# A mixer layer with three branches: splits of attention operands moved to GpSimd, earlier first loads, and new orders

## The chip, the cores and the metric

The kernel runs on one core of a Trainium2 chip. The metric is the device time of one execution in microseconds (us); lower is better. The profile of one execution gives the time of each instruction on each engine: TensorE (PE, with its weight loads as PEld), VectorE (DVE), ScalarE (ACT), GpSimd (POOL) and SyncE (SP), which issues nearly all DMAs here. PEclk, or granted clock, is the share of full speed that TensorE was given in a stretch.

## The reference

One layer with three parallel branches over 256 context tokens ("C") and 2048 latent tokens (a grid of 32 rows by 64 columns; four blocks of 512 tokens, L0 to L3).

```python
h = rmsnorm(x, g_pre) * (1.0 + scale) + shift          # scale, shift, gate = linear(silu(cond))
proj = h @ w_in                                        # 1024 -> 8208 columns
# A: gated DeltaNet, forward and backward, chunked, short conv on q, k, v; 4 heads of 128
# B: attention, 8 heads of 64: latents see an 8 x 16 neighbourhood plus all 256 context keys
#    in one softmax, with a bias table; context tokens see context tokens
# C: centred pooling with windows 2, 4, 8, 16, then a 128 x 128 product per group
y_na = o_na * silu(proj[..., OFF_NA_Z:OFF_PL_U])
merged = g_dn * (y_dn @ w_br_dn) + g_na * (y_na @ w_br_na) + g_pl * (y_pl @ w_br_pl)
out = x + gate * rmsnorm(merged @ w_out, g_post)
```

Outputs: both token sets, the context keys and values of branch B, and the final DeltaNet states of the context. Everything is in float32.

## The kernel before

A large product is made of three fp32r products: each operand is split into a high part (a cast to fp32r) and a low part (operand minus high part), and high-high, high-low and low-high are summed (`mm3`). So each operand needs a cast and a subtraction before TensorE can use it.

**Stages.** (1) Start: the modulation comes from `w_ada` in four parts of 2 MB (`ada_part`, q = 0 to 3, two tiles of 1 MB each, in a ring of three buffers), the inputs are normalised and transposed (`norm_x`, `turn`), and `make_h` writes the high and low part of h for C, L0 and L1. The first two weight units (`load_w`: 128 columns of `w_in`, two pieces of 256 KB, each with a cast and a subtraction on GpSimd) are loaded during q = 2 and q = 3. (2) `qkv` for C, L0, L1, then for L2, L3. (3) `rest`: the 40 other column units, first over C, L2, L3, then, after `reload_h` has fetched h of L0 and L1 again into the buffers of L2 and L3 (hL0 and hL1), over L0, L1. (4) `final`: the branch products, gates, output product and norm for L2, L3, L1, L0, C in turn; `final_y` loads and splits the branch outputs of a block (tiles yo, yh, yl).

**The side chain.** During `rest` the generator `branches` runs: gates of DeltaNet, preparation of 18 token tiles (`dn_prep`, `dn_invert`, `dn_merge`), the scan (`dn_scan`), then attention (`na_blocks`, `na_lane`, `na_pair`), then `final_y("L2")`, one after the other. Its matmuls are placed among the projections' by a hand-kept clock `self.t`: each matmul adds its modelled length, each piece of side work yields the model time at which it wants to go on, and `poll` emits it when that time has come. TensorE executes what results strictly in this order; the projections (tile mm, from hL0 and hL1) are the filler between side matmuls. The order of the other engines is made by a scheduler; loads issued through `dma_here` keep their order in SP's queue.

**The lines around the change.** `prep_load` starts the four loads of a tile and returns the model time at which the tile may be used:

```python
return Q, Qv, Es, self.t + 6
```

In attention, a group is one pair of heads with its keys (1536 latent and context columns, or 256 for C); it serves two blocks of queries (one for C), and a block is worked off in 4 jobs (2 for C) by three lanes. `na_pump` hands out loads whenever a buffer came free: queries of the next block, keys of the next group, values, bias tables, in that order, and again until nothing changes. Queries of a block are only asked for once the keys of its group have been. `split_part` loads up to 512 columns into a tile raw (two buffers) and splits them:

```python
self.nc.scalar.copy(hi, rv)
self.nc.gpsimd.tensor_tensor(lo, rv, hi.bitcast(F32), ALU.subtract)
self.use("s", n / 1000)
self.use("g", n / 400, self.t + 3)
```

`use` books modelled time on an engine; a block may start at the end of what is booked on GpSimd. At the end of a block its output oT is multiplied on GpSimd by the gate path z, for which raw is used once more, and stored.

Of the kernel before, what the change touches and what calls it, by code (L numbers as in the profile page):

```python
# [7 lines left out]
F32 = mybir.dt.float32  # L8
# [8 lines left out]
P = 128  # L17
# [30 lines left out]
class Net:  # L48
# [135 lines left out]
    def run(self):  # L184
        tc = self.tc
        with ExitStack() as st:
# [12 lines left out]
            with ExitStack() as s1:  # L199
                self.hp = pool(s1, "hp")  # L200
                self.wp = pool(s1, "wp", 3)
                with ExitStack() as s2:
                    self.ring("ax", s2, 6)
                    hcs = ExitStack()
                    self.dcs = ExitStack()
                    self.dc = phase(self.dcs, "dc", 1)
                    self.hc = phase(hcs, "hc", 1)
                    with ExitStack() as s3:
                        self.st = phase(s3, "st")
                        hA, hB = {}, {}  # L210
                        xp = phase(s3, "xp")
                        with ExitStack() as s4:
                            self.ap = phase(s4, "ada", 4)
                            self.xp, self.x_bufs = self.ap, 6
                            xc = self.norm_x(self.load_x("C", self.dma_here))
                            self.ada_start()
                            ws, tc_, t0, self.h0 = [], [], [], []
                            self.turn(xc, [xp.tile([P, D], F32, name="x", bufs=4) for _ in range(2)], tc_, range(KT))
                            hc = self.make_h("C", xc, hA, tc_)
                            for q in range(4):  # L220
                                self.ada_part(q)
                                if q == 0:
                                    x0 = self.norm_x(self.load_x("L0", self.dma_here))
                                    xt = [self.ap.tile([P, D], F32, name="xt") for _ in range(4)]
                                    h0 = self.make_h("L0", x0, hA, t0)
                                if q < 2:
                                    self.turn(x0, xt, t0, range(4 * q, 4 * q + 4))
                                else:
                                    ws.append(self.load_w(C_QKV + (q - 2) * P, self.dma_here))
                                for h in (hc, hc, h0, h0):  # L230
                                    next(h, None)
                            self.xp, self.x_bufs = xp, 4
                            x1 = self.load_x("L1", self.dma_here)
                            for h in (hc, h0):
                                next(h, None)
                            for k in range(KT):
                                self.dma_here(self.d_h["L0"][:, k, :], self.h0[k])
                            first = ws, [self.proj(w, hA["C"], CTX, self.ax1()) for w in ws]
                        self.lend(2)
                        self.more_consts()  # L240
                        self.qp = phase(s3, "qp")
                        self.norm_x(x1, tc.keep_in_program_order)
                        self.t += 6
                        self.add(self.make_h("L1", x1, hA), "h")
                        self.t -= 6
                        self.add(self.bias_tables())
                        self.qkv(hA, False, hB, first)
                        self.drain()
                        self.qkv(hB, True, None)
                        self.drain()  # L250
                    self.ax_es = s2.pop_all()
# [200 lines left out]
    def ada_part(self, q):  # L452

        nc = self.nc
        ps = self.mm_bank()
        for s in range(2):
            t = self.ap.tile([P, KT, 256], F32, name="w_ada", bufs=3)
            self.dma_here(t.rearrange("p k n -> p (k n)"), self.a["w_ada"][s, q])
            for k in range(KT):
                for c in range(2):  # L460
                    self.mm(ps[64 * s + 32 * c:64 * s + 32 * c + 32, :P], self.ada_sc[:, k, :], t[:, k, c * P:(c + 1) * P], k == 0, k == KT - 1)
        r = self.wp.tile([P, 4, P], F32, name="wraw", bufs=3)[:, 0]
        nc.scalar.copy(r, ps[:, :P])
        tp = self.ax1()[:, :P]
        self.tr(tp, r, self.ident)
# [334 lines left out]
    def prep_load(self, t):  # L800
# [8 lines left out]
        for d in (0, 1):  # L809
            E = dp.tile([P, 4, P], F32, name="E")  # L810
            self.dma(E, bass.AP(self.d_gr.tensor, self.d_gr.offset + (t * 8 + 4 * d) * P, [[0, P], [P, 4], [1, P]]))
            Es.append(E)
        return Q, Qv, Es, self.t + 6

    def dn_prep(self, t, ti, ub, Ms, ld):
        nc, dp = self.nc, self.dp
# [321 lines left out]
    def rest(self, h, blocks):  # L1138
# [4 lines left out]
        groups = [units[0:2]] + [[u] for u in units[2:-2]] + [units[-2:]]  # L1143
        for g in groups:
            ws = [self.load_w(u[0]) for u in g]
            for b in blocks:
                for w, (_, out, args) in zip(ws, g):
                    out(self.proj(w, h[b], BLK[b]), b, BLK[b], *args)

# [98 lines left out]
    def split_part(self, srcs, hi, lo, view=lambda x: x):  # L1248

        n = sum(s.shape[-1] for s in srcs)  # L1250
        raw = self.np.tile([P, 512], F32, name="raw", bufs=2)
        c = 0
        for s in srcs:
            self.dma(raw[:, c:c + s.shape[-1]], s)
            c += s.shape[-1]
        rv = view(raw[:, :n])
        self.nc.scalar.copy(hi, rv)
        self.nc.gpsimd.tensor_tensor(lo, rv, hi.bitcast(F32), ALU.subtract)
        self.use("s", n / 1000)
        self.use("g", n / 400, self.t + 3)  # L1260

    def na_blocks(self):

        self.blocks, self.groups = [], []
        for base, rbs in ((None, ("C",)), (0, (0, 1)), (12, (2, 3))):
            for hp in range(4):
                g = dict(base=base, hp=hp, left=len(rbs) * (2 if base is None else 4), ready=1e9)
                for rb in rbs:
# [9 lines left out]
    def na_pump(self):  # L1278

        while True:  # L1280
            n = self.group_n, self.block_n, self.v_n, self.tab_n
            g, b = self.group_n, self.block_n
            if b < len(self.blocks) and (b < 2 or self.blocks[b - 2]["scored"] == self.blocks[b - 2]["jobs"]):
                if self.blocks[b]["g"]["ready"] < 1e9:
                    self.na_queries(self.blocks[b])
                    self.block_n += 1
            if g < len(self.groups) and (g < 2 or self.groups[g - 2]["left"] == 0) and self.block_n >= (0, 1, 2, 3, 4, 6, 8, 10, 12, 14, 16, 18)[g] - 1:
                self.na_keys(self.groups[g])
                self.group_n += 1
            if self.v_n < len(self.v_queue):  # L1290
                old = self.v_queue[self.v_n - VBUFS] if self.v_n >= VBUFS else None
                if old is None or old[0]["read"][old[1]] == 2:
# [70 lines left out]
    def na_pair(self, lane, b, cb):  # L1363
# [101 lines left out]
        b["done"] += 1  # L1465
        if b["done"] == b["jobs"]:
            d = "C" if rb == "C" else f"L{rb}"
            while (1, hp, d) not in self.z_there:
                yield self.t + 1
            z = np_.tile([P, 512], F32, name="raw", bufs=2)[:, :BLK[d]]  # L1470
            self.dma(z, self.d_z[d][1, :, hp, :])
            nc.gpsimd.tensor_tensor(oT[:, :BLK[d]], oT[:, :BLK[d]], z, ALU.mult)
            self.dma(self.d_o[1, d][:, hp, :], oT[:, :BLK[d]])
        self.na_pump()

# [12 lines left out]
    def final_y(self, b, dma=None):  # L1488
# [3 lines left out]
        for bi in range(3):  # L1492
            yh = f.tile([P, 4, 512], F32R, name=f"yh{bi}", bufs=1)
            yl = f.tile([P, 4, 512], F32R, name=f"yl{bi}", bufs=1)
            for k in range(4):
# [5 lines left out]
                else:  # L1501
                    src = self.d_pl["L"][k, :, int(b[1]) * 512:(int(b[1]) + 1) * 512]
                dma(o[:, :n], src)
                if bi == 2:
                    z = f.tile([P, 512], F32, name="yz")
                    dma(z[:, :n], self.d_z[b][bi, :, k, :])
                    self.nc.gpsimd.tensor_tensor(o[:, :n], o[:, :n], z[:, :n], ALU.mult)
# [160 lines left out]
```

## Time and profile before

| | us |
|---|---|
| median of 3 runs | 2852.83 (2845.39 to 2856.17) |
| the profiled execution's own time | 2854.77 |
| its span | 2853.1 |
| TensorE busy in the span | 2764.9 (97%) |
| VectorE, ScalarE, GpSimd busy | 1477.3, 875.6, 1163.5 |

The span is what the trace covers; the execution's own time is 1.7 us longer. The mean granted clock is 0.987. TensorE's busy time is the union of its matmuls, whose ends are modelled. 64% of the span on the chain that ended last is TensorE at line 167 (all matmuls) on tiles mm, ax and sx; tile ax holds products of DeltaNet and some projections, sx those of attention, fo the output product.

### The profile page before, as it was taken

How to read it: one execution, taken by the hardware profiler on the slowest of the kernel's cores; microseconds unless marked ns; L12 is line 12 of the kernel's file. 1: busy time of each engine (PE TensorE's matmuls, PEld its weight loads, DVE VectorE, ACT ScalarE, POOL GpSimd, SP SyncE). 2: the span in 40 equal slices, each digit the busy share in tenths (PEclk: the TensorE clock that was granted, in tenths of full speed). 3: DMA queues.
4: the chain of work that ended last, by engine and by line, in shares of the span. 5: the costliest groups of instructions: out<-in, count | busy, mean ns of one | idle time of the engine just before them, and what ended most of it. 6: DMA issues, size and time to landing. Idle time of an engine off the chain costs nothing.

```text
span 2853.1 us, 49537 instructions
## 1 busy us (share of the span) xinstructions
PE 2764.9 (97%) x18254; PEld 2348.7 (82%) x18254; DVE 1477.3 (52%) x3128; ACT 875.6 (31%) x2145; POOL 1163.5 (41%) x1478
## 2 busy tenths in 40 slices
PE   6999999999999999999899999899999999999998
PEld 5888998888788888888788988688878877778887
DVE  6750055201488564655724665266666636446445
ACT  5221132112333232313223355344444422121112
POOL 4523233431334243323422056543333246656643
PEclk9999999999999999999999999999999999999999
DMA  7745423433555363645458986555555366556544
GB/s 285 212 137 174 144 98 96 119 96 112 184 166 158 122 214 108 202 126 161 142 184 302 313 281 215 177 156 151 168 148 159 108 207 233 184 174 217 175 156 135
DMA packets 354116, 492.26 MB, mean 173 GB/s; under 512 B 74921, under 2 KB 192721, under 8 KB 352849
## 3 DMA queue, kind: packets, MB, share of 16 engines
q1 hardware_dynamic: 353872, 489.09, 53.9%
q8 instruction: 144, 2.36, 0.3%
q14 instruction: 100, 0.81, 0.1%
HBM read 347.13 MB, written 155.60 MB: 176 GB/s over the span
## 4 chain that ended last, share of the span: by engine, by line
PE 73%; DMA 8%; DVE 8%; issue 3%; POOL 3%; ACT 2%; SPq 1%; POOLq 0%; ACTq 0%; DVEq 0%
PE mm L167 35%; PE ax L167 24%; PE sx L167 5%; PE fo L167 4%; PE sx L171 3%; PE ax L171 1%; DVE tm L917 1%; DVE Y L918 1%; DMA yo<-d_o0L 1%; DMA d_of<-o 1%; DMA yo<-d_o1L 1%; DMA raw<-d_nkL 1%; DVE mt L891 1%; DMA yz<-d_zL 1%; SPq L151 1%
## 5 line engine op out<-in xcount | busy, mean ns | idle before, releaser
L585 POOL CAST whi<-wraw 128x512 fp32r<-128x512 f32 x240 | 157.5, 657 | 625.2 <-PE ax L167 320.9
L167 PE MATMUL mm<-hL0h,whi 128*128 128x512 f32 x784 | 326.0, 416 | 2.9 <-ACT hL0h L181 2.9
L586 POOL TENSOR_TENSOR wlo<-wraw,whi 128x512 fp32r<-128x512 f32 x240 | 319.6, 1333 | 15.0
L167 PE MATMUL mm<-hL0l,whi 128*128 128x512 f32 x784 | 309.1, 394 | 1.6 <-POOL hL0l L182 1.6
L167 PE MATMUL mm<-hL0h,wlo 128*128 128x512 f32 x784 | 309.2, 394 | 0.0
L167 PE MATMUL mm<-hL1h,whi 128*128 128x512 f32 x472 | 197.7, 419 | 3.8 <-ACT zc L1155 3.8
L167 PE MATMUL ax<-hL1h,whi 128*128 128x512 f32 x488 | 195.4, 400 | 0.0
L167 PE MATMUL ax<-hL1l,whi 128*128 128x512 f32 x488 | 191.6, 393 | 1.8 <-DVE hL1l L548 1.1
L167 PE MATMUL ax<-hL1h,wlo 128*128 128x512 f32 x488 | 191.1, 392 | 0.0
L167 PE MATMUL mm<-yh,br_l 128*128 128x512 f32 (+1 forms) x480 | 179.2, 373 | 9.5 <-POOL br_l L1535 8.6
L167 PE MATMUL mm<-hL1h,wlo 128*128 128x512 f32 x472 | 186.0, 394 | 0.0
L167 PE MATMUL mm<-hL1l,whi 128*128 128x512 f32 x472 | 185.9, 394 | 0.0
L167 PE MATMUL mm<-yh,br_h 128*128 128x512 f32 (+1 forms) x480 | 178.0, 371 | 2.0 <-DVE gt L1542 1.0
L167 PEld LDWEIGHTS mm<-hL0h,whi 128*128 128x128 f32 x784 | 149.2, 190 | 35.4 <-issue 5.6
L167 PE MATMUL mm<-yl,br_h 128*128 128x512 f32 (+1 forms) x480 | 177.8, 370 | 0.0
L167 PEld LDWEIGHTS mm<-hL0h,wlo 128*128 128x128 f32 x784 | 148.6, 190 | 32.5
L167 PEld LDWEIGHTS mm<-hL0l,whi 128*128 128x128 f32 x784 | 149.4, 191 | 27.4 <-POOL hL0l L182 2.1
L1535 POOL TENSOR_TENSOR br_l<-br_r,br_h 128x512 fp32r<-128x512 f32 x104 | 149.6, 1450 | 0.7
L1408 DVE CUSTOM_DVE_ANT_0 pr<-sx,tab 128x736 f32<-128x736 f32 (+2 forms) x128 | 105.7, 863 | 81.7 <-PE sx L167 72.7
L1410 ACT ACTIVATE pr<-pr,mx 128x736 f32<-128x736 f32 (+2 forms) x128 | 109.5, 856 | 109.2 <-DVE mx L1408 109.0
L167 PE MATMUL fo<-woh,mh 128*128 128x512 f32 x288 | 113.9, 396 | 7.2 <-DVE fy L1581 7.2
L167 PEld LDWEIGHTS mm<-yh,br_l 128*128 128x128 f32 x480 | 91.8, 191 | 27.7 <-POOL br_l L1535 11.5
(383 smaller groups left out, 6787.4 us busy)
## 6 DMA issues: line engine op xcount, KB each, us to landing
wraw<-w_u SPq DMA_DIRECT2D x240, 256.0 KB
br_r<-w_br SPq DMA_DIRECT2D x120, 256.0 KB
d_gL<-th SPq DMA_DIRECT2D x96, 256.0 KB
gt<-d_gL SPq DMA_DIRECT2D x96, 256.0 KB
skv<-d_kv SPq DMA_DIRECT2D x36, 512.0 KB
d_zL<-zc SPq DMA_DIRECT2D x48, 256.0 KB
tab<-d_tab SPq DMA_DIRECT2D x48, 240.0 KB
V<-d_nvL SPq DMA_DIRECT2D x128, 80.0 KB
```

Of the source, the lines that this page charges most:

```text
L151: return self.nc.sync.dma_start(out, in_)
L167: self.nc.tensor.matmul(out, lhsT=l, rhs=r, start=start, stop=stop)
L171: self.nc.tensor.transpose(out, in_, ident)
L585: self.nc.gpsimd.tensor_copy(h, raw)
L586: self.nc.gpsimd.tensor_tensor(l, raw, h.bitcast(F32), ALU.subtract)
L891: v.transpose(mt[q, h], M[q, h, q])
L917: v.tensor_tensor(tv, U[:n, 0:i, i:i + 1].broadcast_to([n, i, w]), Y[:n, i:i + 1, i:32].broadcast_to([n, i, w]), ALU.mult)
L918: v.tensor_tensor(Y[:n, 0:i, i:32], Y[:n, 0:i, i:32], tv, ALU.subtract)
L1408: nc.vector.tensor_tensor_reduce(out=pr[:, :nk], in0=ps[:, :nk], in1=tab[0][hh][:, :nk], scale=-1.0, scalar=3e38, op0=ALU.add, op1=ALU.min ...
L1410: nc.scalar.activation(pr[:, :nk], pr[:, :nk], AF.Exp, bias=mx, scale=-1.0, accum_out=sm)
L1535: nc.gpsimd.tensor_tensor(wl, raw, wh.bitcast(F32), ALU.subtract)
```

## The change

Six edits, all in the order or place of work; no product is added or left out.

1. Start: the first two weight units are loaded during q = 1 and q = 2. The `w_ada` tiles of q = 1 and 2 lie in the still unused h buffers of L1, those of q = 0 and 3 in a ring of two; the small row r gets a tile of its own, where it had taken a buffer of the weights' ring.
2. The first DeltaNet tile may be used 14 us of model time after its loads, the others 6 as before.
3. In `rest`, the last group of units (two units) goes over C last.
4. `split_part` casts on GpSimd; the booked time becomes n / 250 in two pieces.
5. Attention takes L2, L3 before L0, L1, and `na_pump` asks for keys, then queries, then values and tables.
6. The gate path of the context's attention output is multiplied in `final_y`, as the pooling branch's is, no longer at the end of the context's attention blocks.

```diff
                                 if q < 2:
                                     self.turn(x0, xt, t0, range(4 * q, 4 * q + 4))
-                                else:
-                                    ws.append(self.load_w(C_QKV + (q - 2) * P, self.dma_here))
+                                if q in (1, 2):
+                                    ws.append(self.load_w(C_QKV + (q - 1) * P, self.dma_here))
...
         ps = self.mm_bank()
+        if q in (1, 2):
+
+            both = self.hp.tile([P, KT, 512], F32R, name="hL1h" if q == 1 else "hL1l").bitcast(F32)
+            both = both.rearrange("p k n -> p (k n)").rearrange("p (s k n) -> p s k n", s=2, k=KT)
         for s in range(2):
-            t = self.ap.tile([P, KT, 256], F32, name="w_ada", bufs=3)
+            t = both[:, s] if q in (1, 2) else self.ap.tile([P, KT, 256], F32, name="w_ada", bufs=2)
...
-        r = self.wp.tile([P, 4, P], F32, name="wraw", bufs=3)[:, 0]
+        r = self.st.tile([P, P], F32, name="ada_row", bufs=1)
...
-        return Q, Qv, Es, self.t + 6
+        return Q, Qv, Es, self.t + (14 if t == 0 else 6)
...
-            for b in blocks:
+
+            for b in blocks if g is not groups[-1] else sorted(blocks, key=lambda b: b == "C"):
...
-        self.nc.scalar.copy(hi, rv)
+        self.nc.gpsimd.tensor_copy(hi, rv)
         self.nc.gpsimd.tensor_tensor(lo, rv, hi.bitcast(F32), ALU.subtract)
-        self.use("s", n / 1000)
-        self.use("g", n / 400, self.t + 3)
+        self.use("g", n / 250, self.t + 3, 2)
...
-        for base, rbs in ((None, ("C",)), (0, (0, 1)), (12, (2, 3))):
+        for base, rbs in ((None, ("C",)), (12, (2, 3)), (0, (0, 1))):
...
+            if g < len(self.groups) and (g < 2 or self.groups[g - 2]["left"] == 0) and self.block_n >= (0, 1, 2, 3, 4, 6, 8, 10, 12, 14, 16, 18)[g] - 1:
+                self.na_keys(self.groups[g])
+                self.group_n += 1
             if b < len(self.blocks) and (b < 2 or self.blocks[b - 2]["scored"] == self.blocks[b - 2]["jobs"]):
                 if self.blocks[b]["g"]["ready"] < 1e9:
                     self.na_queries(self.blocks[b])
                     self.block_n += 1
-            if g < len(self.groups) and (g < 2 or self.groups[g - 2]["left"] == 0) and self.block_n >= (0, 1, 2, 3, 4, 6, 8, 10, 12, 14, 16, 18)[g] - 1:
-                self.na_keys(self.groups[g])
-                self.group_n += 1
...
-            while (1, hp, d) not in self.z_there:
-                yield self.t + 1
-            z = np_.tile([P, 512], F32, name="raw", bufs=2)[:, :BLK[d]]
-            self.dma(z, self.d_z[d][1, :, hp, :])
-            nc.gpsimd.tensor_tensor(oT[:, :BLK[d]], oT[:, :BLK[d]], z, ALU.mult)
+            if rb != "C":
+                while (1, hp, d) not in self.z_there:
+                    yield self.t + 1
+                z = np_.tile([P, 512], F32, name="raw", bufs=2)
+                self.dma(z, self.d_z[d][1, :, hp, :])
+                nc.gpsimd.tensor_tensor(oT, oT, z, ALU.mult)
...
-                if bi == 2:
+                if bi == 2 or bi == 1 and b == "C":
                     z = f.tile([P, 512], F32, name="yz")
```

## Rows read from the trace of the kernel before

**Rows 1.** Windows by stage: busy PE, PEld, DVE, ACT, POOL; clock, DMA share, GB/s.

```profile
0.00:75.00 75.00, 52.28 (x458) 43.17 (x458) 48.69 (x81) 36.45 (x67) 37.83 (x67) 0.98 0.79 288
...
1800.00:1860.00 60.00, 50.36 (x295) 36.42 (x297) 22.59 (x67) 22.82 (x63) 32.91 (x53) 0.94 0.58 171
1860.00:2290.00 430.00, 424.68 (x3971) 347.05 (x3969) 280.55 (x686) 198.12 (x432) 148.21 (x201) 1.00 0.50 146
...
2342.00:2440.00 98.00, 88.16 (x374) 70.55 (x373) 59.43 (x68) 22.71 (x39) 59.30 (x54) 0.98 0.66 220
```

**Rows 2.** Waits of PE, whole span: us in total, times, longest.

```profile
PE ax L171 <- DVE x L518: 13.4, 6, 8.8
...
PE sx L167 <- DVE oT L1463: 4.7, 4, 1.6
PE ax L171 <- DMA Q<-d_dnC: 4.2, 1, 4.2
...
PE mm L167 <- DMA w_ada<-w_ada: 2.7, 2, 1.6
```

**Rows 3.** Windows around four waits of PE, columns as in the first group.

```profile
746.60:752.10 5.50, 5.47 (x19) 4.92 (x20) 3.32 (x9) 4.99 (x20) 1.01 (x2) 0.50 0.83 291
1373.50:1383.40 9.90, 5.39 (x14) 3.66 (x13) 9.76 (x12) 4.00 (x7) 7.82 (x7) 0.66 0.68 216
...
1808.50:1821.60 13.10, 7.45 (x28) 5.17 (x28) 2.45 (x8) 3.25 (x10) 6.14 (x11) 0.74 0.76 210
...
1854.00:1856.00 2.00, 0.81 (x14) 0.81 (x16) 0.80 (x2) 1.41 (x5) 1.24 (x2) 1.00 0.56 174
```

**Rows 4.** VectorE from 20 to 50, shapes apart: count, busy us, mean ns, idle.

```profile
L547 DVE TENSOR_SCALAR x<-xt,ada_A,ada_mod 128x512 f32<-128x512 f32 x4 | 4.1, 1020 | 0.0
...
L547 DVE TENSOR_SCALAR hf<-xt,ada_A,ada_mod 128x512 f32<-128x512 f32 x4 | 2.2, 541 | 0.0
```

**Rows 5.** GpSimd's timeline at the first weight unit: start, length, idle before.

```profile
36.30 1.42 POOL L585 CAST whi<-wraw 128x512 fp32r<-128x512 f32 x2
```

**Rows 6.** The chain that ended last, before DeltaNet's first tile: start, length.

```profile
741.68 4.81 DMA Q<-d_dnC
```

**Rows 7.** Timelines of SP and PE at the reload of L0.

```profile
1373.07 0.90 SPq L151 DMA_DIRECT2D th<-d_hL  x2
...
1377.26 0.80 PE L167 MATMUL mm<-hL0h,whi 128*128 128x512 f32 x1 [2.90 <-ACT hL0h L181]
1379.66 0.80 PE L167 MATMUL mm<-hL0l,whi 128*128 128x512 f32 x1 [1.61 <-POOL hL0l L182]
```

**Rows 8.** Timelines of SP and PE at the start of attention.

```profile
1806.53 0.62 SPq L151 DMA_DIRECT2D raw<-d_nkC  x1
...
1810.70 0.43 SPq L151 DMA_DIRECT2D raw<-d_nqC  x1
...
1814.21 0.58 PE L167 MATMUL sx<-khi,qhi 64*128 64x256 f32 x2 [5.64 <-ACT qhi L1257]
```

**Rows 9.** Timelines of POOL and DVE inside attention.

```profile
1910.98 1.53 POOL L586 TENSOR_TENSOR wlo<-wraw,whi 128x512 fp32r<-128x512 f32 x1
...
1911.67 1.67 DVE L1421 TENSOR_SCALAR pr<-pr,rs 128x608 f32<-128x608 f32 x1
...
1917.33 0.54 DVE L1421 TENSOR_SCALAR pr<-pr,rs 128x608 f32<-128x608 f32 x1
```

**Rows 10.** The casts of `split_part` (line 1257): ns min/median/max, first and last start.

```profile
L1257 ACT CAST khi<-raw x28: 401/620/625, 1809.1 to 2178.7; 128x512 fp32r<-128x512 f32 x24, 128x256 fp32r<-128x256 f32 x4
...
L1257 ACT CAST qhi<-raw x20: 404/619/621, 1813.8 to 2225.9; 128x512 fp32r<-128x512 f32 x16, 128x256 fp32r<-128x256 f32 x4
```

**Rows 11.** End of attention and of the filler: timelines of SP, PE and DVE.

```profile
2290.03 0.88 SPq L151 DMA_DIRECT2D yo<-d_o0L  x2
...
2323.93 0.39 PE L167 MATMUL mm<-yh,br_h 128*128 128x512 f32 x1
...
2329.39 0.39 PE L167 MATMUL mm<-yh,br_h 128*128 128x512 f32 x1
...
2328.72 2.14 DVE L182 TENSOR_TENSOR yl<-yo,yh 128x512 fp32r<-128x512 f32 x2 [5.54 <-ACT yh L181]
```

## Prediction

> **What bounds the kernel now.** The table of engine times is read first: TensorE is busy 2764.9 of 2853.1 us, so 88 us of idle is all that a change of order can take, plus what a slow clock adds. The windows by stage say where that idle lies [rows 1]: 22.7 us in the first 75, 9.6 where attention starts (1800 to 1860), only 5.3 in the 430 us of attention's body, 9.8 in the first 98 us of the final stage; the rest is spread thin. The waits of TensorE, read next, give the idle names [rows 2]; of the edits' own places there are 2.7 us on `w_ada`, 4.2 on the first Q tile, 4.7 on oT. The largest, 13.4 us on x, belongs to the loads of the inputs, which no edit touches. Last, fine windows show what follows a wait [rows 3]: after the Q tile's wait, 5.5 us ran busy with a granted clock of 0.50, that is 1.2 GHz, so half of it (2.7 us) was lost again; around the reload the mean was 0.66, at attention's start 0.74. But 1854 to 1856 holds 1.2 us of idle in pieces at a clock of 1.00. So each compact wait of some 4 us costs about 7, and a short one only itself.
>
> TensorE executes in order, projections (filler) between the matmuls of the side chain. The second bound is at the end of this filler [rows 11]: the loads of `final_y` for L2 start at 2290.0, when attention has closed its buffers; the filler's last matmul is at 2323.7, the first on yh at 2323.9. The 24 matmuls of the first two branches pass at 0.23 us each, so the third branch is reached at 2329.4, and its last low part is ready at 2328.72 + 2.14 = 2330.9, about when it is read. The side chain is thus hidden with less than 1 us to spare. Whatever moves it later against the filler comes back as idle there; a stall that goes shortens everything; a stall that goes because the chain is told to come later does not.
>
> **The change, part by part.** Sums are against the profiled execution's own 2854.77 us, which is 1.9 above the median.
>
> *Start.* Tiles in other buffers and earlier units let `w_ada` run ahead: of the 2.7 us of waiting [rows 2] most goes. GpSimd's casts of the units now fall where VectorE has little of make_h to do: at 36.3 GpSimd casts two pieces in 1.42 us [rows 5], and in that stretch four VectorE operations took 1020 ns where four of the same form took 541 [rows 4], 1.9 us in all. The weight loads also move ahead of two `w_ada` parts in SP's queue: 1 MB more before parts of 8 MB, hidden while the transfers run ahead of x's wait. The bounds are -6 (2.7 + 1.9, and some of the low clock) and 0 (the wait on x simply ends later work at the same time); I take -4.
>
> *First DeltaNet tile.* The chain before it ends on the Q load, issued 741.7, landed 746.5 [rows 6]. With 8 us more the transposes come at some 750, 4 us after landing: the wait of 4.2 and the half clock of 2.7 go, -6.9. But the chain is now 8 later against the filler, which at the end of the filler is +8 with under 1 of slack: net +1. Bounds: -7 if other waits (`poll` with its booked times) give that shift back, +1 if not. I take +1. If the load is late by more than 8, the old wait stays in part; the row excludes that.
>
> *Context last in the last group.* After the reload TensorE waits 2.9 on hL0h (ScalarE) and 1.6 on hL0l (GpSimd), the clock is 0.66 over 9.9 us [rows 3, 7]. With C last, 48 matmuls of C (two units, 256 columns, about 0.12 us each as half of 0.23) lie behind the last readers of L2's and L3's h, and SP's loads of th, first at 1373.07, may go 5.8 us earlier. That exceeds 4.5, so the wait would go, and 5.4 busy at 0.66 against full speed is about 2.6. Bounds -7.1 and 0 (the split is queued on ScalarE or VectorE behind the side chain's own work, as it comes at the same time); I take -5.
>
> *Attention's start.* SP issues the keys' load at 1806.53, then values and tables, the queries' at 1810.70; TensorE waits 5.64 for qhi [rows 8]. Keys before queries before the rest brings the queries' load some 3 us ahead; the wait falls to about 2, short enough to keep the clock: -3.5, and the low clock's cost: 7.45 busy at 0.74 lost 1.9 [rows 3], with the rest of the slow stretch behind it about 3. The 4 us of smaller idle that is left in [rows 1] loses perhaps 2. Against it, the booked time rises from n / 400 to n / 250, which lets C's blocks begin later by some 3 (an estimate from the code: 0.77 for a split of 512, over four groups of small ones), paid at the filler's end. Net -5.5, bounds -12 and -3 (only the order of two loads).
>
> *Splits.* 48 casts leave ScalarE, 40 of 0.62 and 8 of 0.40 us [rows 10], 28 us. It is off the path: 198 of 430 us busy [rows 1]. They go to GpSimd at 0.71 for 512 columns [rows 5], about 31 us, on top of 148 of 430. GpSimd has the room; the danger is VectorE, which is busy 281. Beside a GpSimd operation of 1.53 us a VectorE one took 1.67 where the next of its form took 0.54 [rows 9]: up to 1.1 us held for each meeting. VectorE is not the path, except where oT is waited for (4.7 us [rows 2]). Against that, high and low part now come from one queue with no hand-over between engines. Bounds -5 (all waits of the body) and +5 (the waits on oT doubled); I take -1.
>
> The Trainium skill ("Trainium Architecture — The Big Picture", section "What this means for kernel authors") says that VectorE and GpSimd share a pair of ports under an exclusive lock, not a split of bandwidth. The trace agrees so far (1.67 against 0.54 us). By that rule alone, with the lock's time on the path, the sum would be that of rival D.
>
> *Order of the halves, gate in `final_y`.* 0 each. Loads, tables and products are the same in number; the jobs come in another order. L2 is still the first block of `final`, and its attention output now exists half a stage earlier. The four multiplications by z for C are moved from attention to the last block's `final_y`, on GpSimd, with four loads in SP's queue; what covers them are the output products of L0, the block before; without this cover they would cost their load and four operations, some 8 us by the latency of [rows 6] and 0.7 us each.
>
> *End of the filler.* Its shift is already in the terms. Idle there lets the branch weights' splits run ahead, so the 9.8 us of 2342 to 2440 may shrink: 0, bounds -7 and +3.
>
> Sum: -4 + 1 - 5 - 5.5 - 1 = -14.5, so 2840.3 on the profile's time and **2838** for the median.
>
> **Rivals.**
>
> *A, the sum:* 2838, own range 2827 to 2848.
>
> *B, the filler's end does not bind:* if the chain's model times absorb the 8 and the 3, as `poll` can emit two pieces closer, those 11 us come off: 2838 - 11 = 2827, about 2828. For it: the loads and splits of `final_y` (2290 to 2331, 41 us) hold gaps of 5.5 us [rows 11]. Against it: the 8 are added at the first of many strictly successive tiles.
>
> *C, the waits reappear:* the reload's splits meet VectorE's and ScalarE's work for the side chain, now 8 us later; the queries are early but wait behind the low part of the keys on GpSimd. Then of reload and attention's start only 1 stays and the start gives its lower half: some -5, so 2848. For it: the reload's waits are of ScalarE and GpSimd, not of a load [rows 7], and attention's of a cast [rows 8]. Against it: both casts follow their load directly.
>
> *D, slower:* GpSimd's casts in attention hold the softmax's VectorE work, and that the softmax's matmuls, one for one: +31, so 2869. For it, the meeting in [rows 9]; against it, 5.3 us of idle in 430, so slack exists. It changes the sign from 14.5 / 48 = 0.30 us per cast, and is a clear loss from (14.5 + 14.3) / 48 = 0.60.
>
> **How the numbers follow.** A 0.50, B 0.20, C 0.23, D 0.07. About 0.5% (14.3 us: 2838.6 to 2867.1) is what can be told from no change. A lies on this border, so its half is split, 0.27 faster, 0.23 same; B is all faster; C is nearly all same (0.20), a small part faster (0.03); D is slower (0.06) with 0.01 same. Faster 0.50, same 0.44, slower 0.06. The range reaches from below B's value to above C's, 2822 to 2853; it leaves out D and the low tail, where B meets the bound of -12 at attention's start.
>
> **What would show it.** Start: no wait on `w_ada`, the first `qkv` matmuls some 4 us earlier. First tile: no wait on Q, clock 1.00 there. Reload: th issued 5 us sooner after the last L3 matmul, no wait over 2 on hL0h. Attention: a wait on qhi of about 2, clock near 1.00; line 1257 on GpSimd at about 0.7; VectorE's line 1421 at a mean not much above now. End: 5 to 11 us of idle between the last filler matmul and those on yl. The last is the test of A against B: without that idle, and with the rest as said, the time is B's. The prediction is wrong if the body's idle grows past 20 us (D), or if the first tile's missing wait is found again at the reload or at attention's start (C).

## The result: slower by 0.6%

| | before | changed |
|---|---|---|
| median, us | 2851.55 (2845.39 to 2860.60, 6 runs) | 2869.57 (2863.65 to 2871.52, 6 runs) |
| the profiled execution's own time | 2854.77 | 2869.01 |
| its span | 2853.1 | 2867.3 |

The ratio is 1.0059, 95% interval 1.0044 to 1.0074: 17 us slower, where 2838 was forecast in a range of 2822 to 2853. The value is that of rival D (2869), but by coincidence: as the experiments show, not by its mechanism, and its sign, more than 20 us of idle in attention's body, is not there (3.3 us, below).

**The stages after.** The windows of the changed kernel, columns as in [rows 1]; the second and the last row are stretches that were not looked at before.

```profile
0.00:75.00 75.00, 56.43 (x478) 47.30 (x479) 47.75 (x84) 37.41 (x69) 40.84 (x69) 0.95 0.79 295
900.00:1050.00 150.00, 144.84 (x1096) 124.64 (x1095) 89.95 (x238) 43.40 (x119) 50.06 (x72) 0.94 0.48 149
1800.00:1860.00 60.00, 51.94 (x270) 37.55 (x269) 19.54 (x59) 15.34 (x48) 32.75 (x61) 0.91 0.53 161
1860.00:2290.00 430.00, 426.66 (x3897) 347.84 (x3895) 290.83 (x676) 176.99 (x393) 185.01 (x247) 1.00 0.50 148
2321.00:2361.00 40.00, 24.14 (x55) 14.52 (x56) 17.04 (x19) 8.90 (x13) 18.60 (x17) 0.57 0.64 218
```

Two rows of the kernel before that answer to the second and the last:

```profile
900.00:1050.00 150.00, 146.27 (x1119) 124.72 (x1118) 94.99 (x242) 46.11 (x128) 51.90 (x76) 0.98 0.48 153
2324.00:2364.00 40.00, 34.69 (x150) 27.41 (x149) 22.29 (x26) 7.73 (x10) 25.55 (x23) 1.00 0.64 206
```

The start is fuller by 4.2 us (56.4 busy against 52.3), at a clock of 0.95 against 0.98. Attention's start has 8.1 us of idle where it had 9.6, at a clock of 0.91 against 0.94: nothing gained. Attention's body is not hurt: 3.3 us of idle in 430, where it had 5.3 [rows 1]. The great difference is the last row: in the 40 us behind the end of the filler TensorE worked 24.1 us at a clock of 0.57, where it had worked 34.7 us at full speed.

**The waits after.** TensorE's waits over the whole span: us in total, times, longest; those of before are in [rows 2].

```profile
PE mm L167 <- ACT yh L181: 9.5, 3, 4.3
PE mm L167 <- POOL br_l L1540: 8.0, 3, 4.8
PE ax L167 <- DVE Tc L938: 6.0, 2, 4.2
...
PE mm L167 <- ACT zc L1160: 5.3, 1, 5.3
PE mm L167 <- POOL wlo L590: 4.4, 1, 4.4
PE sx L167 <- POOL qhi L1262: 4.3, 2, 2.9
```

The wait on the first Q tile is gone, and those on oT and hL0h too. In their place stand Tc (6.0, in the merge of DeltaNet's inverted blocks), wlo (4.4, at the reload), zc (5.3, where 3.8 had been waited before) and, largest, yh. The wait on br_l, the low part of the branch weights, is in all about what it was (8.0 against 8.6), but 4.8 of it now stand at the end of the filler. The next rows, of three timelines of the changed kernel, show this end and answer to [rows 11]. SP's first loads of the final stage:

```profile
2311.64 0.88 SPq L151 DMA_DIRECT2D yo<-d_o0L  x2
```

TensorE, with the idle time just before each in brackets:

```profile
2320.88 0.80 PE L167 MATMUL mm<-yh,br_h 128*128 128x512 f32 x1 [2.36 <-POOL br_h L1539]
...
2330.53 0.77 PE L167 MATMUL mm<-yh,br_h 128*128 128x512 f32 x1 [4.78 <-POOL br_l L1540]
...
2342.74 0.80 PE L167 MATMUL mm<-yh,br_h 128*128 128x512 f32 x1 [3.27 <-ACT yh L181]
...
2351.65 0.80 PE L167 MATMUL mm<-yh,br_h 128*128 128x512 f32 x1 [4.32 <-ACT yh L181]
```

VectorE's last low part:

```profile
2351.63 1.92 DVE L182 TENSOR_TENSOR yl<-yo,yh 128x512 fp32r<-128x512 f32 x2 [1.80 <-ACT yh L181]
```

The loads start 21.6 us later than before (2311.6 against 2290.0), while the filler ends 3 us earlier (first matmul on yh at 2320.9 against 2323.9). The filler left behind attention had shrunk from some 36 us to 12 (9 of work, the rest a wait), and the third branch came at 2342.7 instead of 2329.4. The four matmuls shown last 0.77 to 0.80 us, where the same ones of before took 0.39 at full clock.

**A ledger.** Starts of four events in the tile views of Q, sx and yh, and the end of the span. As TensorE's work up to the first matmul on yh is the same in every version (15950 matmuls in each trace, give or take one), the column "first yh" says what was won or lost up to the filler's end, and the last one what was lost behind it. These are single executions: the versions that leave 33.6 us of filler or more, experiment 12 aside, have last columns from 523.7 to 529.2, so less than some 5 us there is not told from scatter.

| | first Q transposes | last Q | first scores | last sx | first yh | filler left (yh - sx) | yh to the end |
|---|---|---|---|---|---|---|---|
| before | 746.6 | 1347.0 | 1814.2 | 2287.5 | 2323.9 | 36.4 | 529.2 |
| changed | 745.6 | 1353.4 | 1816.8 | 2309.2 | 2320.9 | 11.7 | 546.4 |
| 1: booking only | 745.4 | 1343.3 | 1804.0 | 2301.2 | 2322.0 | 20.8 | 540.9 |
| 3: changed, old times | 742.3 | 1344.8 | 1803.0 | 2281.9 | 2315.6 | 33.7 | 523.7 |
| 4: changed, old booking | 745.7 | 1357.1 | 1814.4 | 2293.3 | 2314.7 | 21.4 | 532.6 |
| 5: wait of 14 only | 750.4 | 1365.6 | 1831.9 | 2305.0 | 2329.1 | 24.1 | 530.1 |
| 8: 3 without the context last | 742.7 | 1341.6 | 1797.1 | 2277.4 | 2311.1 | 33.7 | 527.0 |
| 9: 8 with booking n / 600 | 742.8 | 1340.9 | 1795.1 | 2291.0 | 2311.1 | 20.1 | 538.9 |
| 12: 8 with a wait of 3 | 743.4 | 1359.0 | 1814.5 | 2288.1 | 2327.2 | 39.1 | 521.7 |

The changed kernel: 3.0 us won up to the filler's end, 17.2 lost behind it, 14.2 in all.

### The profile page after: what moved, and what is told of

Same layout as the page of the kernel before. It is cut to its first block, busy times and chain, and to the rows that moved or that the text cites. A ratio compares the mean times of both kernels' runs of the same rounds, so it can differ in the third digit from the quotient of the medians.

```text
span 2867.3 us, 49508 instructions
## 1 busy us (share of the span) xinstructions
PE 2776.0 (97%) x18254; PEld 2354.2 (82%) x18254; DVE 1501.0 (52%) x3128; ACT 848.5 (30%) x2097; POOL 1194.3 (42%) x1526
## 4 chain that ended last, share of the span: by engine, by line
PE 77%; DVE 9%; DMA 6%; POOL 2%; issue 2%; ACT 2%; SPq 1%; POOLq 0%; DVEq 0%; ACTq 0%
PE mm L167 38%; PE ax L167 25%; PE sx L167 6%; PE fo L167 4%; PE sx L171 3%; DVE tm L921 2%; DVE Y L922 2%; PE ax L171 1%; SPq L151 1%; DMA yo<-d_o0L 1%; DMA yz<-d_zL 1%; DVE yl L182 1%; DMA yo<-d_o1L 1%; DMA br_r<-w_br 1%; DVE ps_s L1210 1%
## 5 line engine op out<-in xcount | busy, mean ns | idle before, releaser
L167 PEld LDWEIGHTS mm<-yh,br_h 128*128 128x128 f32 x480 | 92.8, 193 | 37.3 <-ACT yh L181 12.2
```

Source lines behind the costliest of these rows:

```text
L167: self.nc.tensor.matmul(out, lhsT=l, rhs=r, start=start, stop=stop)
```

## The experiments

The theories: (1) the later times of the side chain use up the filler before the final stage's operands are there; (2) rival D, GpSimd's casts hold VectorE. The filler that a version leaves behind attention can also be counted in the order in which its instructions stand, since TensorE keeps to it; where an expectation gives such a number, the trace gave it within 3 us (the column above).

| | ratio to before | 95% interval |
|---|---|---|
| changed | 1.0059 | 1.0044 to 1.0074 |
| 1: before + booking n / 250 | 1.0061 | 1.0046 to 1.0076 |
| 2: before + casts on GpSimd | 0.9984 | 0.9972 to 0.9995 |
| 3: changed, old booking and wait of 6 | 0.9962 | 0.9949 to 0.9975 |
| 4: changed, old booking | 1.0004 | 0.9991 to 1.0018 |
| 5: before + wait of 14 | 1.0026 | 1.0015 to 1.0037 |
| 6: before + new start | 0.9966 | 0.9953 to 0.9979 |
| 7: 3 with the old order of halves | 0.9975 | 0.9962 to 0.9988 |
| 8: 3 without the context last | 0.9952 | 0.9935 to 0.9969 |
| 9: 8 with booking n / 600 | 1.0014 | 1.0000 to 1.0028 |
| 10: 8 with the old order of loads | 0.9969 | 0.9958 to 0.9980 |
| 11: before + new start + casts | 0.9970 | 0.9957 to 0.9982 |
| 12: 8 with a wait of 3 | 0.9997 | 0.9985 to 1.0010 |

**1, the booking alone**

```diff
-        self.use("s", n / 1000)
-        self.use("g", n / 400, self.t + 3)
+        self.use("g", n / 250, self.t + 3, 2)
```

> The kernel before, with only the booked time of a split changed to n / 250 in two pieces; no instruction is added, removed or moved to another engine, only the order in which TensorE meets attention's matmuls. In this order 20.5 us of projections are left behind attention's last matmul, where before had 36.2 and the changed kernel 8.9 (512-column products counted at 0.2275 us each). Theory 1 (the chain's later booked times use up the filler): idle of 5 to 15 us and a half clock between the filler's last matmul and the third branch of the final stage, time +8 to +16 us against before. Theory 2 (GpSimd's casts hold VectorE): no cast has moved, so within 3 us of before.

Slower by 0.61% (2867.78), as much as the whole change. No instruction was added or moved between engines. In the ledger the side chain's end has come 13.7 us later, the filler left is 20.8, and 11.7 us are lost behind it: the 40 us from the first matmul on yh on (2322) are in this row; the clock of 0.79 is its third number from the right.

```profile
2322.00:2362.00 40.00, 27.24 (x97) 19.70 (x96) 21.90 (x24) 9.24 (x13) 19.41 (x18) 0.79 0.60 196
```

**2, the casts alone**

```diff
-        self.nc.scalar.copy(hi, rv)
+        self.nc.gpsimd.tensor_copy(hi, rv)
```

> The kernel before, with only the 48 casts moved from ScalarE to GpSimd; booked times as before, so TensorE's order is that of before. Theory 1: within 4 us of before. Theory 2: the casts are the loss, +10 to +31 us.

Faster by 0.16% (about 5 us). Theory 2 is refuted as the cause. Whether the casts hold VectorE can be looked for in the softmax multiplication of the largest shape, here from 1860 to 2270 in five kernels (count, busy us, mean ns, idle before it). Before:

```profile
L1421 DVE TENSOR_SCALAR pr<-pr,rs 128x736 f32<-128x736 f32 x64 | 48.8, 764 | 1.6
```

Changed, with the cast:

```profile
L1425 DVE TENSOR_SCALAR pr<-pr,rs 128x736 f32<-128x736 f32 x56 | 49.6, 886 | 1.7
...
L1262 POOL CAST khi<-raw 128x512 fp32r<-128x512 f32 x22 | 13.9, 643 | 34.2 <-DMA raw<-d_nkL 20.2 <-PE sx L167 13.9
```

Experiment 2:

```profile
L1421 DVE TENSOR_SCALAR pr<-pr,rs 128x736 f32<-128x736 f32 x64 | 52.4, 819 | 1.7
```

Experiment 3:

```profile
L1426 DVE TENSOR_SCALAR pr<-pr,rs 128x736 f32<-128x736 f32 x60 | 43.1, 721 | 1.5
```

Experiment 1, which moves no cast:

```profile
L1420 DVE TENSOR_SCALAR pr<-pr,rs 128x736 f32<-128x736 f32 x62 | 53.8, 868 | 1.8
```

Two pairs have the same order on TensorE and differ by the casts alone: before and experiment 2 (764 and 819 ns), and experiments 6 and 11 (759 and 817). So the casts hold this operation by some 0.06 us a time, and the time of this experiment says that this is off the path; VectorE is busy 291 of 430 us in the body of the changed kernel. The 886 of the changed kernel can't be put down to the casts: experiment 1 has 868 without them, experiment 3 has 721 with them, so the order of the instructions moves this mean more than the casts do. The cast itself takes 0.64 us. The Trainium skill ("Trainium Architecture — The Big Picture", section "What this means for kernel authors") has VectorE and GpSimd share one pair of ports under an exclusive lock. The two pairs agree with it in direction (+55 and +58 ns).

**3 and 4, the change with the old times.** In 3 the booking of before and 6 for the first tile, in 4 the booking alone; everything else as changed.

```diff
-        return Q, Qv, Es, self.t + (14 if t == 0 else 6)
+        return Q, Qv, Es, self.t + 6
-        self.use("g", n / 250, self.t + 3, 2)
+        self.use("s", n / 1000)
+        self.use("g", n / 400, self.t + 3)
```

> The changed kernel with the old booking (n / 400 and n / 1000) and 6 for the first DeltaNet tile; GpSimd still casts, the start, the reload order, the halves and the gate are as changed. 33.5 us of filler are left behind attention's last matmul. Theory 1: the 17 us that the changed kernel lost behind the end of the filler shrink to 2 or less, and the wait on the first Q tile comes back with 4 to 7 us: 2853 to 2860, about 12 us under the changed kernel. Theory 2: the casts are still there, so within 4 us of the changed kernel.

> The changed kernel with the old booking alone; the first DeltaNet tile still waits 14. 21.2 us of filler are left. Theory 1: by the loss of 17.2 us for 27.3 us of lost filler, 15.0 us of lost filler cost about 9.5, and no wait on Q comes back: 2859 to 2864, some 8 us under the changed kernel. Theory 2: within 4 us of the changed kernel.

3 is faster than before by 0.38% (2840.98) and 4 is like before (2854.59); both are faster than expected (2853 to 2860, and 2859 to 2864). For 4 the expectation took the loss behind the filler as proportional to the filler that is missing; at 21.4 us left it was 3.4 instead of 9.5. So the booking costs 0.55% (about 16 us) inside the change and the wait 0.42% (12 us); without both, the rest gains 11. In 3, the filler left is 33.7, and the first 40 us of the final stage run at full clock:

```profile
2315.60:2355.60 40.00, 37.33 (x159) 29.08 (x157) 25.38 (x30) 7.75 (x10) 28.58 (x25) 1.00 0.66 215
```

**5, the wait alone**

```diff
-        return Q, Qv, Es, self.t + 6
+        return Q, Qv, Es, self.t + (14 if t == 0 else 6)
```

> The kernel before, with only the first DeltaNet tile's 14 instead of 6. 23.9 us of filler are left behind attention's last matmul instead of 36.2. Theory 1: the wait on Q (4.2 us and a half clock, 7 in all) goes, and the end of the filler is short by 12: idle and a half clock between the filler's last matmul and the third branch, +3 to +10 us against before. The rival that the wait's removal counts in full: -7 us, and no idle at the filler's end.

Slower by 0.26% (7 us), inside the forecast, but not by its reason: although 12 us of filler were missing (24.1 left), only 0.9 us was lost behind it, and 5.2 before it (first yh at 2329.1 against 2323.9). That loss shows in the preparation: from the first to the last Q it took 615.2 us where before took 600.4. The new wait is that on Tc. In the changed kernel's timeline of TensorE it is this row:

```profile
954.29 3.43 PE L167 MATMUL ax<-Tc,M 32*32 32x32 f32 x64 [4.21 <-DVE Tc L938]
```

In experiment 5, by the waits of TensorE from 900 to 1050:

```profile
PE ax L167 <- DVE Tc L934: 4.3, 1, 4.3
```

The rows of 700 to 760 in the changed kernel and before:

```profile
700.00:760.00 60.00, 60.00 (x351) 48.98 (x344) 21.24 (x47) 17.34 (x45) 20.83 (x27) 1.00 0.55 176
...
700.00:760.00 60.00, 55.76 (x308) 44.50 (x307) 18.56 (x41) 16.04 (x41) 20.08 (x27) 0.94 0.50 155
```

60.0 us busy at a clock of 1.00, where before had 55.8 at 0.94: 4.2 + 3.3 = 7.5 us won at the first tile. But 900 to 1050 has 1.4 us more idle and a clock of 0.94 against 0.98: 144.8 x 0.06 - 146.3 x 0.02 = 5.8, so 7.2 us lost, 200 us later. That the 14 move VectorE's work under the inversion, on which Tc depends, is argued and was not tried.

At the end of the filler experiment 5 lost 9 us more than before in the first 40 (30.9 busy at 0.83, against 34.7 at 1.00), and won nearly all of it back later: behind these 40 us it was idle for 3 us less (the wait on fy is 3.3 us shorter), and the mean clock up to the end was 0.99 against 0.98, some 5 us. Experiment 5, the 40 us, the rest of the span, and the wait:

```profile
2329.00:2369.00 40.00, 30.88 (x115) 23.18 (x114) 24.43 (x26) 8.61 (x12) 23.14 (x21) 0.83 0.55 182
...
2369.00:2859.20 490.20, 471.51 (x2193) 393.31 (x2191) 261.64 (x330) 87.11 (x179) 276.07 (x274) 0.99 0.56 185
...
PE fo L167 <- DVE fy L1581: 3.9, 3, 1.7
```

The kernel before, the rest of the span and the wait:

```profile
2364.00:2853.10 489.10, 467.56 (x2157) 389.80 (x2155) 257.67 (x326) 85.84 (x177) 271.85 (x269) 0.98 0.56 181
...
PE fo L167 <- DVE fy L1581: 7.2, 3, 4.0
```

**6, the start alone**

```diff
-                                    ws.append(self.load_w(C_QKV + (q - 2) * P, self.dma_here))
+                                if q in (1, 2):
+                                    ws.append(self.load_w(C_QKV + (q - 1) * P, self.dma_here))
...
+            t = both[:, s] if q in (1, 2) else self.ap.tile([P, KT, 256], F32, name="w_ada", bufs=2)
```

> The kernel before, with only the start changed. By the prediction's term: -4 us (0 to -6), seen as more TensorE busy time in the first 75 us. The rival: as the wait on the inputs ends at the same time, within 1 us of before.

Faster by 0.34% (10 us, 6 to 13), more than expected. TensorE is 56.4 us busy in the first 75. The wait on `w_ada` is not what went; the waits on VectorE's hf, hCl and hL1l are (4.2 us before, 0.5 now; 0.7 on GpSimd's hL1l is new). Its waits in the first 75 us:

```profile
PE mm L167 <- DMA w_ada<-w_ada: 2.9, 1, 2.9
...
PE ax L167 <- POOL hL1l L552: 0.7, 1, 0.7
PE ax L171 <- DVE hf L551: 0.5, 1, 0.5
```

The two groups of operations of which one had a mean of 1020 ns [rows 4]; now neither has:

```profile
L551 DVE TENSOR_SCALAR hf<-xt,ada_A,ada_mod 128x512 f32<-128x512 f32 x4 | 2.5, 614 | 0.0
L551 DVE TENSOR_SCALAR x<-xt,ada_A,ada_mod 128x512 f32<-128x512 f32 x4 | 2.2, 541 | 0.0
```

Of the 10 us, 5.1 are seen at the first Q transposes (741.5 against 746.6); the rest could not be placed, as single executions differ by as much (below).

**7, the halves, and 8, the context last.** Both are experiment 3 with one order undone.

```diff
-        for base, rbs in ((None, ("C",)), (12, (2, 3)), (0, (0, 1))):
+        for base, rbs in ((None, ("C",)), (0, (0, 1)), (12, (2, 3))):
```

> The third experiment's kernel (changed, with the old booked times), with the halves of attention in their old order. 36.2 us of filler are left instead of 33.5. By the prediction's term of 0 for the order: within 2 us of the third experiment's 2841. The rival: the 2.7 us of filler count, up to 3 us faster.

```diff
-            for b in blocks if g is not groups[-1] else sorted(blocks, key=lambda b: b == "C"):
+            for b in blocks:
```

> The third experiment's kernel, with the context again ahead of the other blocks in the last group of units before the reload. By the prediction's term: 5 us slower than the third experiment, as the loads of th come 5 us later and the wait on hL0h grows by that much. The rival, from the third experiment's profile, where hL0h was still waited for 4.3 us: the loads are held by something else, and the order is worth less than 2 us.

7: 0.9975 against 0.9962, intervals that overlap; the order of the halves is worth nothing that can be told. 8: 0.9952, so the 5 us that the context last should gain are not there; by the two ratios it costs 0.1% (3 us), with intervals that overlap. The traces show why there is no gain. SP's loads of th (the last parts of h) share a ring of three buffers with the gates' results, and the two gates of C now stand in front of them. These timelines answer to [rows 7]. TensorE's last product with L3's h, in experiment 3 and in experiment 8:

```profile
1361.58 0.39 PE L167 MATMUL mm<-hL1h,wlo 128*128 128x512 f32 x1
...
1363.87 0.39 PE L167 MATMUL ax<-hL1h,wlo 128*128 128x512 f32 x1
```

SP in experiment 3:

```profile
1369.09 0.43 SPq L151 DMA_DIRECT2D d_gC<-th  x1
1373.19 0.32 SPq L151 DMA_DIRECT2D th<-d_hL  x1
```

SP in experiment 8:

```profile
1367.03 1.23 SPq L151 DMA_DIRECT2D th<-d_hL  x2
```

SP in the changed kernel:

```profile
1366.49 0.32 SPq L151 DMA_DIRECT2D d_gC<-th  x1
1366.90 0.64 SPq L151 DMA_DIRECT2D th<-d_hL  x1
```

TensorE in the changed kernel, the wait that took the place of that on hL0h:

```profile
1372.26 0.79 PE L167 MATMUL mm<-hL0h,wlo 128*128 128x512 f32 x1 [4.39 <-POOL wlo L590]
```

With C last, the first load of th follows the store of C's gate (d_gC). It comes 11.6 us after the last product with L3's h in 3 and 9.8 in the changed kernel (1357.1 to 1366.9); with C first, 3.2 us in 8 and 3.9 before (1369.2 to 1373.1). So the h buffers of L3 were free and the load still did not go. That the ring of th held it is read from the order of SP's queue and was not tried by itself. In the changed kernel hL0h was no longer waited for, but the low part of the next weights was, for 4.4 us, where before had 4.5 on hL0h and hL0l.

**9, a smaller booking**

```diff
-        self.use("g", n / 400, self.t + 3)
+        self.use("g", n / 600, self.t + 3)
```

> The eighth experiment's kernel (all of the change but the later wait, the booking and the context last; 2835) with a split booked at n / 600 instead of n / 400: a smaller price than either version. In the built order 19.8 us of filler are left behind attention's last matmul, where the eighth had 33.5. Theory 1 as the prediction had it (the booked prices of the splits add up): a smaller price lets attention end earlier, so the same time or less. Theory 1 in a second form (a booked price shifts the phase in which the three lanes, the loads and the projections interleave; either side of the tuned n / 400 slips): about 14 us less filler, +8 to +15 us against the eighth.

Slower than 8 by 0.6% (1.0014 against 0.9952, some 18 us): a lower price costs as much as a higher one. The ledger has it in the same places as experiment 1: against 8, attention ends 13.6 us later and 11.9 us are lost behind the filler. So the cost is not the price times 48 splits. That n / 400 happens to be a good phase of three lanes, loads and filler, from which both neighbours slip, fits the three values tried; the phase itself was not looked at.

**10, the order of loads in attention.** Experiment 8 with the queries asked for ahead of the keys again, in `na_pump`:

```diff
-                self.na_keys(self.groups[g])
-                self.group_n += 1
...
                     self.na_queries(self.blocks[b])
                     self.block_n += 1
...
+                self.na_keys(self.groups[g])
+                self.group_n += 1
```

> The eighth experiment's kernel with the old order of loads in attention (queries, keys, values, tables). By the prediction's term for attention's start (the wait falls from 5.6 to 2 and the slow stretch goes): +4 to +8 us against the eighth, and a wait of some 5.6 on the queries. The rival: the wait is cut in two and moves to the low parts, so within 2 us.

0.9969 against 0.9952, about 5 us by the two ratios, with intervals that overlap, so a gain is likely and not shown. The waits of TensorE from 1795 to 1830 say where it would lie: the queries are waited for 6.1 us in 10 and 2.0 in 8. Experiment 10:

```profile
PE sx L167 <- POOL qhi L1262: 6.1, 1, 6.1
```

Experiment 8:

```profile
PE sx L171 <- ACT pr L1410: 2.8, 3, 1.2
PE sx L167 <- POOL qhi L1262: 2.0, 1, 2.0
```

The 60 us around the first scores (14 before them, 46 behind), first of 8, then of 10:

```profile
1783.10:1843.10 60.00, 50.13 (x262) 35.24 (x260) 22.40 (x63) 14.86 (x46) 31.24 (x59) 0.91 0.56 158
...
1788.80:1848.80 60.00, 48.26 (x258) 34.23 (x256) 19.83 (x62) 14.53 (x46) 28.98 (x54) 0.89 0.49 148
```

Idle and slow clock together (60 less busy times clock) are 14.4 us in 8, 17.0 in 10 and, by [rows 1], 12.7 before: the shorter wait on the queries helps against 10, but the stretch is no better than before, and its clock is 0.91 although no wait in it is longer than 2.0 us.

**11, start and casts.** The kernel before with the edits of experiments 6 and 2 together.

> The kernel before with the new start and the casts on GpSimd, nothing else. If the parts add: 2850 - 10 - 4 = 2836, -11 to -16 us against before; if the casts' gain and the start's are the same time counted twice: -10.

Faster by 0.30% (8 us): no more than the start alone, so the two gains don't add, or the casts' is nearer to the lower end of its interval.

**12, an earlier first tile**

```diff
-        return Q, Qv, Es, self.t + 6
+        return Q, Qv, Es, self.t + 3
```

> The eighth experiment's kernel with 3 for the first DeltaNet tile instead of 6; 38.9 us of filler are left instead of 33.5. If filler at the end still pays: down to -4 us against the eighth. If the end has enough and the wait on Q only grows by the 3 that the chain comes earlier: +1 to +4 us.

Slower than 8 by 0.45% (13 us), against both expectations. The filler left is largest of all (39.1), and behind it 521.7 us are the least of all; but the preparation took 615.6 us where 8 took 598.9. Three waits stand out, on Q and Tc in the preparation and on hL0l behind it, at the reload:

```profile
PE ax L171 <- DMA Q<-d_dnC: 7.9, 1, 7.9
...
PE mm L167 <- POOL hL0l L182: 6.2, 1, 6.2
...
PE ax L167 <- DVE Tc L938: 4.0, 2, 2.6
```

So, at the values tried (3, 6 and 14), the chain's start loses by a shift to either side, as the booking does (n / 600, n / 400, n / 250).

## Why the prediction was wrong

**The step that failed** is the size of the shift against the filler. The prediction took 8 us for the tile and "some 3" for the booking, 11 in all. Counted in the order of the instructions, the filler left behind attention fell by 27.3 us, from 36.2 to 8.9: 2.7 by the order of the halves (36.2 in experiment 7, 33.5 in 3), 12.3 by the wait of 14 (21.2 in 4; the same 12.3 alone in 5), and 12.3 by the booking (8.9 in the changed kernel; 15.7 alone in 1). The trace has 24.7 between attention's end and the first matmul on yh (36.4 to 11.7), since 2.4 of the 11.7 are a wait. The booking was costed as a price, 0.77 us for a split over four small groups; it acts as a change of order, and its size and even its sign cannot be had from the price (experiment 9). The second bound itself was right: the end of the filler is where the time was lost, 17.2 us against a net loss of 14.2, in waits and at half clock, as the part on what bounds the kernel had it.

**Less than 1 us to spare** was wrong in the other direction. The first 12 us of missing filler cost 0.9 us behind it (experiment 5), which is within the scatter; with 15 missing it was 3.4 (experiment 4) and 11.7 (experiment 1), with 27 it was 17.2 (the changed kernel). So the filler that is left puts the versions in order, but does not give the loss. In the 40 us behind the filler's end experiment 5 does lose 9, but some 8 of it come back later: the term that the prediction put at 0, with a bound of -7. The prediction had expected this of the branch weights' splits; it came in the wait on fy and in the clock, while br_l was waited for as long as before in this part (4.7 against 4.5 us).

**The first tile**: the stall and its half clock went as forecast (7.5 for 6.9), and came back whole as the wait on Tc. This is rival C's kind of loss, in a place that the prediction did not name. The term of +1 was +7 alone and +12 inside the change.

**The start**: -4 was -10 (-6 to -13); the part on VectorE's stretch was the right one, the part on `w_ada` was not. **The reload**: -5 was nothing to +3; the h buffers of L3 were free and did not bring the loads sooner, as the ring of th stood in the way (read from the queue, not tried). One number of its sum was also off: 5.39 busy at 0.66 lose 1.8 us by the working used elsewhere, not 2.6, so the bound was -6.3. **Attention's start**: the wait fell to 2.0 us, as forecast, when the old times were kept (experiment 8), but the low clock did not go with it (0.91, where before had 0.94): other short waits took its place. Of the 8.5 us about 5 came against the old order of loads (experiment 10), by intervals that overlap; in the changed kernel qhi was waited for twice, 4.3 us in all, with 1.5 on the low part of the keys between, as rival C had said, and the gain was nothing. "A short one only itself" therefore held for the one stretch of [rows 3] and not here. **The casts**: -1 was about -5 alone (-1 to -8), of which nothing was seen on top of the start (experiment 11); D's mechanism is excluded. **The halves**: 0 was not contradicted in time, though they took 2.7 us of filler. The gate in `final_y` was not tried by itself.

The whole, by the path over experiments 3 and 4. All edits but the two times: forecast -18.5 (-4, -5, -8.5, -1), measured -11. The wait of 14: forecast +1, measured +12. The booking: forecast +3, measured +16. The gains were overrated by two thirds of themselves, and the two costs came to 28 where 4 had been put down.

What stays open: why DeltaNet's preparation slips by 7 to 17 us when its start is moved either way, which is seen in Tc's wait and the clock behind it but was not taken apart; which part of the booking edit, the price, its two pieces or the dropped booking of ScalarE, turns the order; and where the other half of the start's gain lies. The best version is experiment 8, 0.48% faster than before (0.31 to 0.65%): the change without the context last, with the old booking and a wait of 6.

## What to carry to other kernels

Where a hand-kept clock decides the order of one engine, a changed estimate is a changed order: before anything is costed, count in the new order how much filler is left behind the side chain, since that is a number that no price gives. Here, a stall that was removed by telling a chain to come later was found again further on. And where a buffer ring is shared, look at what else stands in it before an order is chosen to free another buffer sooner.

## What was not expected of the hardware

What a wait costs in slow clock differs between executions of the same instructions. The kernel before and experiment 1 have the same order up to attention, and both wait 3.6 to 3.8 us on zc at some 1415. In the 80 us from the end of that wait TensorE was busy throughout, and the clock was 0.92 in the one and 0.96 in the other: 6.4 against 3.2 us lost. Experiment 1 reached attention 10 us before the other (1804.0 against 1814.2). Single profiles can therefore not place a gain of a few us far downstream; the ratios of several runs can tell that there is one. The window of before:

```profile
1418.60:1498.60 80.00, 79.98 (x687) 65.98 (x688) 21.69 (x28) 19.51 (x35) 21.28 (x22) 0.92 0.54 181
```

Of experiment 1:

```profile
1414.40:1494.40 80.00, 80.00 (x701) 66.51 (x702) 21.27 (x28) 20.09 (x36) 20.43 (x21) 0.96 0.58 195
```
